# Last down products in column halves, and attention's small loads on the weights' queue

## The chip, the cores and the metric

One core of a Trainium2 chip runs the whole program. The metric is the device time of one execution in microseconds (us); three runs of the kernel before took 1378.57, 1380.28 and 1381.85, the median being 1380.28. The engines are TensorE (PE; PEld is its weight load), VectorE (DVE), ScalarE (ACT), GpSimd (POOL) and SyncE (SP), which here issues transfers. Each engine works through its own stream of instructions in order, and they meet at semaphores.

## The reference

Two pre-norm residual layers on x of 256 tokens by 1024 columns, with adaLN: for each layer, six vectors of 1024 (two shifts, two scales, two gates) come from `silu(c) @ ada_w + ada_b`.

```python
h = rmsnorm(x, norm_mix_w[layer]) * (1.0 + sc1) + sh1
y = hybrid_mixer(h, ...) if layer % 2 == 0 else diff_attention(h, ...)
x = x + g1 * y
h = rmsnorm(x, norm_ffn_w[layer]) * (1.0 + sc2) + sh2
f = swiglu(h, ...) if layer % 2 == 0 else moe_swiglu(h, ...)   # 8 experts, top 2
x = x + g2 * f
```

Layer 0 has the mixer (gated DeltaNet and S5) and a dense SwiGLU with D_FF = 2816; layer 1 has differential attention and the experts. Attention uses a few small parameters: weights of 64 for the norms of q and k (q also takes 1/8), a weight of 128 for the norm of the output times 1 - lambda_init, and

```python
lam = exp(sum(lq1 * lk1)) - exp(sum(lq2 * lk2)) + lambda_init   # four vectors of 64
p = softmax(s1) - lam * softmax(s2)                              # per head, chunk-causal mask
```

## The kernel before

The program is one long list of instructions, written stage by stage; a planner then orders each engine's stream by its own estimate of when operands are ready and by priorities. `behind(ins)` adds an edge for the planner alone: what is written inside comes after `ins` on the engine of `ins`. `modnorm` and `residual` are written with a high priority.

*Weights.* `raw` (L105) issues a load of 1 MB on SP into one of nine buffers, and the load waits until that buffer is free. `split` (L118) makes a high part (whi, ScalarE, L131) and a low part (wlo, VectorE, L132) of 1024 columns; each product of float32 is done as three products of such parts (L398 to L400 for the projections with weights stationary, L406 to L408 for those with tokens stationary).

*Dense feed-forward* (`dense_ffn`). The 22 blocks of 128 hidden columns (f) run in order: two projections of 24 products each, silu and the product of both, the split of the result (hfT, L1162 and L1163), and, one block later, the down products into four accumulators `acc[tt][n]` (two blocks of 128 tokens by two halves of 512 columns; 12 products for each f). Blocks 20 and 21 are left for one last call of `down`, whose 24 products are written token block by token block. Beside this, VectorE sums chunks of the adaLN weights (`ada_sums`, L280 and L282), which TensorE folds in small products (L301). Then `residual_` is called for eight pieces of 256 columns, token block by token block: VectorE multiplies the accumulator by the gate (L733) and adds to x (L734), and ScalarE takes the squares with their sum (L318).

*Norm* (`modnorm_`). VectorE reduces the sums of squares (sst, L332), GpSimd takes the power (L157, L158), x is scaled into xn (L370, L371), TensorE transposes it (tr, L150), ScalarE applies scale and shift (hf, L385), and VectorE splits this into hT (L387, L388), two of the eight steps of 128 at a time. `self.later` holds the last instruction of ScalarE and of VectorE in this.

*Attention* (`diff_attention`). Ahead of its norm it loads small parameters on ScalarE's queue: four rows into rowsC, then subln, four vectors into lt, and the mask, ten transfers in all; the sums on them follow each load at once (a transpose of rowsC and two copies to wcol, L1190 and L1191; subln times a constant, L1194; four instructions for lambda on VectorE, L1199 to L1205, with an Exp on ScalarE, L1202). The tiles are in the pool that takes the place of the feed-forward's. Then come the norm, the projections of q, k and v, adaLN chunks (one on TensorE, L272; its bias rows adab on SP, L295), the heads and the output projection, woven together by due times. The expert stage follows, with most of the weights.

Of the kernel before, what the change touches and what calls it, by code (L numbers as in the profile page):

```python
# [17 lines left out]
P = 128  # L18
T = 256
NT = 2  # L20
# [54 lines left out]
class Trunk:  # L75
# [326 lines left out]
    def tok3(self, out, hT, k, tt, wh, wl, first, last):  # L402
# [5 lines left out]
        nc.tensor.matmul(out, hT[:, k, 0, s], wl, start=False, stop=last)  # L408
# [718 lines left out]
    def dense_ffn(self):  # L1127
# [8 lines left out]
        def down(steps):  # L1136
            self.mark("ffn_down")
            parts = [self.split(w, D) for f, hf, w in steps]
            for tt in range(NT):
# [32 lines left out]
        down(wait)  # L1172
        for tt in range(NT):
            for n in range(4):
                self.residual(acc[tt][n // 2][:, (n % 2) * 256:(n % 2) * 256 + 256], self.gates[(0, 1)], tt,
                              slice(256 * n, 256 * n + 256))


    def diff_attention(self):
# [4 lines left out]
        for r, n in enumerate(("odd_q_norm_w", "odd_k_norm_w")):  # L1184
            for i in range(2):
                S.dma_start(rC[r:r + 1, i, :], a[n])
        pt = self.ps("ms")
        self.transpose(pt[:, :2], rC.rearrange("r i d -> r (i d)"))
        wcol = ap.tile([P, 2], F32, name="wcol")
        V.tensor_scalar(wcol[:, 0:1], pt[:, 0:1], 0.125, None, op0=ALU.mult)  # L1190
        V.tensor_copy(wcol[:, 1:2], pt[:, 1:2])  # L1191
        sub = ap.tile([P, P], F32, name="subln")
        S.dma_start(sub, a["odd_subln_w"].to_broadcast([P, P]))
        V.tensor_scalar(sub, sub, 1.0 - LAMBDA_INIT, None, op0=ALU.mult)  # L1194
        lt = ap.tile([P, 4, 64], F32, tag="ex", name="lt", bufs=2)
        for i, n in enumerate(("odd_lambda_q1", "odd_lambda_k1", "odd_lambda_q2", "odd_lambda_k2")):
            S.dma_start(lt[:, i, :], a[n].to_broadcast([P, 64]))
        lp = ap.tile([P, 2, 64], F32, tag="ex", name="lp", bufs=2)
        V.tensor_tensor(lp, lt[:, 0::2, :], lt[:, 1::2, :], op=ALU.mult)  # L1199
        ls = ap.tile([P, 2], F32, name="lsum")  # L1200
        V.tensor_reduce(ls, lp, axis=AX.X, op=ALU.add)
        S.activation(ls, ls, AF.Exp)  # L1202
        nlam = ap.tile([P, 1], F32, name="nlam")
        V.tensor_tensor(nlam, ls[:, 1:2], ls[:, 0:1], op=ALU.subtract)
        V.tensor_scalar(nlam, nlam, -LAMBDA_INIT, None, op0=ALU.add)  # L1205
        msk = ap.tile([P, T], F32, name="amask")
        S.dma_start(msk, a["amask"])
        hT, _, _ = self.modnorm(1, 0, ap, ("oT",))
        yT = ap.tile([P, KD, 2, T], F32R, name="oT", tag="oT")
# [627 lines left out]
```

## Time and profile before

| | before |
|---|---|
| time of the profiled execution | 1378.09 us |
| its span, first to last instruction | 1376.3 us |
| median of the timed runs | 1380.28 us |
| mean granted TensorE clock | 0.978 |
| TensorE, VectorE, ScalarE busy | 1281.9, 826.4, 577.1 us |
| read from HBM | 398.11 MB |

The busy time of an engine is the time in which at least one of its instructions ran. The granted clock is the share of TensorE's full speed that the throttle let through. DMA is the mean busy share of 16 DMA engines. The words after an arrow in a row name what ended the idle time ahead of that instruction.

### The profile page before, as it was taken

To read this page: it belongs to the slowest core of one execution; us is meant where nothing else is said; L and a number is where in the kernel's file an instruction comes from. 1 tells how busy PE (TensorE), PEld (TensorE's weight loads), DVE (VectorE), ACT (ScalarE), POOL (GpSimd) and SP (SyncE) were. 2 spreads that over 40 slices of the span, in tenths; PEclk is the share of its full clock that TensorE was granted. 3 is DMA by queue.
4 is the path that set the end of the run, shared out by engine and by line. 5 is a ranking of instruction groups with operands and counts; after the bars stand their busy time and mean duration, and the time that the engine had idled before them with its cause. 6 is when DMAs were issued, how large, how long until landed. Compare 5 with 4: busy or idle time off the path is not lost.

```text
span 1376.3 us, 26749 instructions
## 1 busy us (share of the span) xinstructions
PE 1281.9 (93%) x10928; PEld 941.8 (68%) x10928; DVE 826.4 (60%) x1516; ACT 577.1 (42%) x990; POOL 123.6 (9%) x118
## 2 busy tenths in 40 slices
PE   3999999989999978999999999999998899999975
PEld 2777666779999978998788435786352468835334
DVE  6688767567878878965798413986020089820202
ACT  3553322455444444664778213775010168711000
POOL 3132322000000003341100000000000000000000
PEclk9799999999999999999999999999999999999998
DMA  9834334159788967821899899999999999999995
GB/s 262 268 114 132 111 106 154 62 177 325 247 270 287 293 211 252 271 96 63 334 305 399 305 380 409 405 409 356 391 409 405 408 409 406 409 397 408 408 396 208
DMA packets 196164, 400.98 MB, mean 291 GB/s; under 512 B 14797, under 2 KB 115650, under 8 KB 196034
## 3 DMA queue, kind: packets, MB, share of 16 engines
q1 hardware_dynamic: 189610, 398.00, 78.7%
q10 hardware_dynamic: 6424, 1.19, 0.5%
q8 instruction: 88, 1.44, 0.4%
q14 instruction: 42, 0.34, 0.1%
HBM read 398.11 MB, written 1.05 MB: 290 GB/s over the span
## 4 chain that ended last, share of the span: by engine, by line
PE 46%; DMA 10%; DVE 4%; issue 1%; ACT 1%; SPq 1%; POOL 0%; ACTq 0%; DVEq 0%
PE pab L1731 9%; DMA raw<-in_odd_expert_w 9%; PE py L1782 5%; PE pab L1675 4%; PE pab L1674 4%; PE pab L1676 4%; PE py L1708 2%; PE py L1709 2%; PE py L1707 2%; PE px L1625 2%; DVE wlo L132 1%; PE pqk L398 1%; PE pqk L399 1%; PE pqk L400 1%; PE pth L150 1%
## 5 line engine op out<-in xcount | busy, mean ns | idle before, releaser
L131 ACT ACTIVATE whi<-raw 128x1024 fp32r<-128x1024 f32 (+2 forms) x352 | 347.1, 1001 | 279.8 <-PE pab L399 52.3
L132 DVE TENSOR_TENSOR wlo<-raw,whi 128x1024 fp32r<-128x1024 f32 (+2 forms) x352 | 402.9, 1168 | 72.6 <-ACT whi L131 70.6
L1731 PE MATMUL pab<-raw,xg 128*32 128x512 f32 (+1 forms) x1920 | 194.2, 524 | 10.5 <-DMA raw<-in_odd_expert_w 10.5
L1731 PEld LDWEIGHTS pab<-raw,xg 128*32 128x32 f32 x1920 | 58.2, 109 | 118.8 <-issue 77.5
L1751 DVE TENSOR_TENSOR hb<-hb,pab 128x256 f32<-128x256 f32 (+1 forms) x35 | 12.4, 364 | 171.0 <-ACT hb L1750 170.5
L1675 PE MATMUL pab<-wlo,xg 128*128 128x512 f32 (+1 forms) x288 | 110.3, 383 | 3.6 <-DVE wlo L132 3.4
L1676 PE MATMUL pab<-whi,xg 128*128 128x512 f32 (+1 forms) x288 | 106.4, 377 | 0.0
L398 PE MATMUL pab<-hT,whi 128*128 128x256 f32 x352 | 101.9, 290 | 0.0
L399 PE MATMUL pab<-hT,whi 128*128 128x256 f32 x352 | 100.3, 285 | 0.1
L400 PE MATMUL pab<-hT,wlo 128*128 128x256 f32 x352 | 99.9, 284 | 0.0
L1782 PE MATMUL py<-raw,hTe 128*32 128x256 f32 (+1 forms) x1760 | 83.7, 343 | 10.7 <-DMA raw<-in_odd_expert_w 8.6
L282 DVE SCALAR_TENSOR_TENSOR adas<-raw,condr,adas 128x256 f32<-128x256 f32 x175 | 86.4, 499 | 3.1
L1674 PE MATMUL pab<-whi,xg 128*128 128x512 f32 (+1 forms) x288 | 84.4, 379 | 3.6 <-DVE xg L1632 1.9
L1782 PEld LDWEIGHTS py<-raw,hTe 128*32 128x32 f32 x1760 | 53.4, 112 | 38.0 <-DMA raw<-in_odd_expert_w 12.8
L1802 DVE TENSOR_TENSOR yf<-py,gate 32x256 f32<-32x256 f32 (+1 forms) x48 | 18.0, 374 | 102.3 <-PE py L1782 101.3
L1750 ACT ACTIVATE hb<-pab 128x256 f32<-128x256 f32 (+1 forms) x35 | 11.5, 338 | 155.8 <-PE pab L1731 155.1
L399 PEld LDWEIGHTS pab<-hT,whi 128*128 128x128 f32 x352 | 68.0, 193 | 0.8 <-DVE hT L388 0.5
L398 PEld LDWEIGHTS pab<-hT,whi 128*128 128x128 f32 x352 | 68.1, 193 | 0.3
L400 PEld LDWEIGHTS pab<-hT,wlo 128*128 128x128 f32 x352 | 67.9, 193 | 0.1
L1675 PEld LDWEIGHTS pab<-wlo,xg 128*128 128x128 f32 x288 | 54.3, 189 | 19.4 <-DVE wlo L132 6.3
L1676 PEld LDWEIGHTS pab<-whi,xg 128*128 128x128 f32 x288 | 54.4, 189 | 10.0
L1674 PEld LDWEIGHTS pab<-whi,xg 128*128 128x128 f32 x288 | 51.0, 189 | 13.7 <-ACT whi L131 2.2
(465 smaller groups left out, 2504.4 us busy)
## 6 DMA issues: line engine op xcount, KB each, us to landing
raw<-in_odd_expert_w SPq DMA_DIRECT2D x215, 1024.0 KB
raw<-in_ada_w SPq DMA_DIRECT2D x48, 1024.0 KB
raw<-in_odd_expert_w SPq DMA_DIRECT2D x64, 768.0 KB
raw<-in_even_ffn_w SPq DMA_DIRECT2D x33, 1024.0 KB
raw<-in_odd_w_qkv SPq DMA_DIRECT2D x12, 1024.0 KB
raw<-in_even_w_in SPq DMA_DIRECT2D x10, 1024.0 KB
raw<-in_even_w_out SPq DMA_DIRECT2D x4, 1024.0 KB
raw<-in_odd_w_out SPq DMA_DIRECT2D x4, 1024.0 KB
```

The costliest lines, as they stand in the source:

```text
L131: act = nc.scalar.activation(hs, src, AF.Copy)
L132: dve = nc.vector.tensor_tensor(l, src, hs, op=ALU.subtract)
L282: nc.vector.scalar_tensor_tensor(s, w[:, k, :], self.condr[:, k, 0:1], s, op0=ALU.mult, op1=ALU.add)
L398: nc.tensor.matmul(out, wh[:, o:o + P], hT[:, k, 0, :], start=(k == 0), stop=False)
L399: nc.tensor.matmul(out, wh[:, o:o + P], hT[:, k, 1, :], start=False, stop=False)
L400: nc.tensor.matmul(out, wl[:, o:o + P], hT[:, k, 0, :], start=False, stop=(k == kd - 1))
L1625: PE.matmul(px[:, kk * n:kk * n + n], self.xn[:, tt, k * P:(k + 1) * P], Pt[:, tt, :n], start=(tt == 0), stop=(tt == 1))
L1674: PE.matmul(p[:, :m], xg[:, k, 0, :], wh[:, s], start=(k == 0), stop=False)
L1675: PE.matmul(p[:, :m], xg[:, k, 0, :], wl[:, s], start=False, stop=False)
L1676: PE.matmul(p[:, :m], xg[:, k, 1, :], wh[:, s], start=False, stop=(k == KD - 1))
L1731: PE.matmul(pu[t][32 * g:32 * g + 32], xg[:, k, 32 * t:32 * t + 32], v[:, :, g * n:(g + 1) * n], start=(k == 0 and (t == 0 or n > P)), sto ...
L1782: PE.matmul(py[32 * g:32 * g + 32, t], hs[f][t], v[:, i, g * n:(g + 1) * n], start=(f == 0 and t == 0), stop=(f == NF - 1 and t == 1))
```

## The change

In `dense_ffn`, the last call of `down` is made with `halves`: the products of columns 0 to 511 of blocks 20 and 21, for both token blocks, and then those of columns 512 to 1023, the second half written behind the last product of the first. The eight pieces of the residual follow in the same order: the four of the first half, then the four of the second. In `diff_attention` the ten small transfers are issued on SP's queue, and all the sums on them are gathered in `small()`, which is called after the norm and behind `self.later`, so that its ScalarE and VectorE instructions come after the norm's last ones on these engines. `wcol` and `nlam` become tiles made after the norm. `tok3` returns its last product.

```diff
-        nc.tensor.matmul(out, hT[:, k, 0, s], wl, start=False, stop=last)
+        return nc.tensor.matmul(out, hT[:, k, 0, s], wl, start=False, stop=last)
...
-        def down(steps):
+        def down(steps, halves=False):
             self.mark("ffn_down")
             parts = [self.split(w, D) for f, hf, w in steps]
+            if halves:
+                mm = None
+                for n in range(2):
+                    cs = slice(512 * n, 512 * n + 512)
+                    with self.behind([mm.ins] if mm else ()):
+                        for (f, hf, w), (wh, wl) in zip(steps, parts):
+                            for tt in range(NT):
+                                mm = self.tok3(acc[tt][n], hf, 0, tt, wh[:, cs], wl[:, cs], f == 0, f == NF - 1)
+                return
...
-        down(wait)
-        for tt in range(NT):
-            for n in range(4):
-                self.residual(acc[tt][n // 2][:, (n % 2) * 256:(n % 2) * 256 + 256], self.gates[(0, 1)], tt,
-                              slice(256 * n, 256 * n + 256))
+        down(wait, True)
+        for h in range(2):
+            for tt in range(NT):
+                for n in (2 * h, 2 * h + 1):
+                    self.residual(acc[tt][h][:, (n % 2) * 256:(n % 2) * 256 + 256], self.gates[(0, 1)], tt,
+                                  slice(256 * n, 256 * n + 256))
...
-                S.dma_start(rC[r:r + 1, i, :], a[n])
+                nc.sync.dma_start(rC[r:r + 1, i, :], a[n])
...
-        S.dma_start(sub, a["odd_subln_w"].to_broadcast([P, P]))
-        V.tensor_scalar(sub, sub, 1.0 - LAMBDA_INIT, None, op0=ALU.mult)
+        nc.sync.dma_start(sub, a["odd_subln_w"].to_broadcast([P, P]))
...
-            S.dma_start(lt[:, i, :], a[n].to_broadcast([P, 64]))
+            nc.sync.dma_start(lt[:, i, :], a[n].to_broadcast([P, 64]))
...
-        S.dma_start(msk, a["amask"])
+        nc.sync.dma_start(msk, a["amask"])
         hT, _, _ = self.modnorm(1, 0, ap, ("oT",))
+        wcol, nlam = ap.tile([P, 2], F32, name="wcol"), ap.tile([P, 1], F32, name="nlam")
+
+        def small():
+            pt = self.ps("ms")
+            self.transpose(pt[:, :2], rC.rearrange("r i d -> r (i d)"))
+            V.tensor_scalar(wcol[:, 0:1], pt[:, 0:1], 0.125, None, op0=ALU.mult)
+            V.tensor_copy(wcol[:, 1:2], pt[:, 1:2])
+            V.tensor_scalar(sub, sub, 1.0 - LAMBDA_INIT, None, op0=ALU.mult)
+            lp = ap.tile([P, 2, 64], F32, tag="ex", name="lp", bufs=2)
+            V.tensor_tensor(lp, lt[:, 0::2, :], lt[:, 1::2, :], op=ALU.mult)
+            ls = ap.tile([P, 2], F32, name="lsum")
+            V.tensor_reduce(ls, lp, axis=AX.X, op=ALU.add)
+            S.activation(ls, ls, AF.Exp)
+            V.tensor_tensor(nlam, ls[:, 1:2], ls[:, 0:1], op=ALU.subtract)
+            V.tensor_scalar(nlam, nlam, -LAMBDA_INIT, None, op0=ALU.add)
+
+        with self.behind(self.later):
+            small()
```

## Rows read from the trace of the kernel before

**Rows 1.** The page: busy time of each engine with its share of the span and its instructions, and the chain of work that ended last by engine.

```profile
PE 1281.9 (93%) x10928; PEld 941.8 (68%) x10928; DVE 826.4 (60%) x1516; ACT 577.1 (42%) x990; POOL 123.6 (9%) x118
...
PE 46%; DMA 10%; DVE 4%; issue 1%; ACT 1%; SPq 1%; POOL 0%; ACTq 0%; DVEq 0%
```

**Rows 2.** The table by stretches of time: the stretch in us, its length, then busy us and instructions of PE, PEld, DVE, ACT and POOL, the granted clock, the DMA share and GB/s.

```profile
503.00:509.70 6.70, 0.00 (x0) 0.00 (x0) 4.77 (x15) 5.32 (x19) 0.89 (x2) 0.74 0.01 4
517.40:521.10 3.70, 0.00 (x0) 0.00 (x0) 0.65 (x3) 3.68 (x4) 0.00 (x0) 0.84 0.79 264
521.10:526.60 5.50, 5.25 (x23) 4.96 (x24) 5.50 (x13) 1.92 (x4) 0.00 (x0) 0.50 0.23 67
526.60:550.00 23.40, 22.98 (x194) 22.16 (x194) 21.37 (x39) 8.86 (x14) 10.54 (x8) 1.00 0.95 309
550.00:585.00 35.00, 34.29 (x281) 31.88 (x281) 31.96 (x91) 21.26 (x57) 12.47 (x15) 1.00 0.83 268
526.60:668.00 141.40, 138.02 (x1131) 127.51 (x1130) 101.98 (x284) 79.61 (x203) 43.61 (x48) 0.99 0.55 179
760.00:1376.00 616.00, 571.61 (x5618) 337.58 (x5617) 251.83 (x329) 204.09 (x292) 0.00 (x0) 0.99 0.99 385
```

**Rows 3.** TensorE's instructions in order of time at the feed-forward's last products: start, duration, line, operands. The first row is the first of the last 24, the second the twelfth, the third the small adaLN products between the blocks, the last row the last of the 24.

```profile
496.65 0.48 PE L406 MATMUL facc<-whi,hfT 128*128 128x512 f32 x1
...
499.27 0.39 PE L408 MATMUL facc<-wlo,hfT 128*128 128x512 f32 x1
499.50 0.50 PE L301 MATMUL gvb<-ones,adas 128*128 128x1 f32 x4
...
502.50 0.39 PE L408 MATMUL facc<-wlo,hfT 128*128 128x512 f32 x1
```

**Rows 4.** VectorE in order of time, same place: the low part of the last hfT, the first two and the last two instructions of the residual.

```profile
497.87 0.43 DVE L1163 TENSOR_TENSOR hfT<-h,hfT 128x256 fp32r<-128x256 f32 x1 [0.41 <-ACT hfT L1162]
...
501.55 0.76 DVE L733 TENSOR_TENSOR res<-facc,gate 128x256 f32<-128x256 f32 x2 [1.15 <-PE facc L408]
...
506.21 0.76 DVE L734 TENSOR_TENSOR x<-x,res 128x256 f32<-128x256 f32 x2
```

**Rows 5.** VectorE in order of time at attention's norm: the reduction, the first cast, the sums on subln, wcol and lt with their waits in brackets, the last instruction of hT, and the low part of the second column's weights.

```profile
507.81 0.16 DVE L332 TENSOR_REDUCE sst<-ss 128x2 f32<-128x8 f32 x1 [0.84 <-ACT sqj L318]
...
512.36 0.43 DVE L387 CAST hT<-hf 128x512 fp32r<-128x512 f32 x1 [1.28 <-ACT hf L385]
514.21 0.23 DVE L1194 TENSOR_SCALAR subln<-subln 128x128 f32<-128x128 f32 x1 [1.42 <-DMA subln<-in_odd_subln_w]
...
515.28 0.15 DVE L1190 TENSOR_SCALAR wcol<-ps 128x1 f32<-128x1 f32 x1
...
520.45 0.29 DVE L1199 TENSOR_TENSOR lp<-lt 128x128 f32<-128x128 f32 x1 [4.35 <-DMA lt<-in_odd_lambda_k]
...
522.31 0.69 DVE L388 TENSOR_TENSOR hT<-hf,hT 128x512 fp32r<-128x512 f32 x1
...
523.45 1.22 DVE L132 TENSOR_TENSOR wlo<-raw,whi 128x1024 fp32r<-128x1024 f32 x1
```

**Rows 6.** The same norm at the head of the feed-forward stage, in order of time: the reduction and the last instruction of hT on VectorE, the transposes on TensorE, the first four hf on ScalarE.

```profile
300.54 0.16 DVE L332 TENSOR_REDUCE sst<-ss 128x2 f32<-128x8 f32 x1 [0.84 <-ACT sqj L318]
...
308.99 0.69 DVE L388 TENSOR_TENSOR hT<-hf,hT 128x512 fp32r<-128x512 f32 x1
...
302.54 3.65 PE L150 MATMUL tr<-cst,xn 128*128 128x128 f32 x16 [4.68 <-ACT xn L371]
...
304.09 1.93 ACT L385 ACTIVATE hf<-tr,modc,modc 128x256 f32<-128x256 f32 x4 [0.96 <-PE tr L150]
```

**Rows 7.** The table by stretches for the products of L398 alone, one of the three in each step of a projection: length, busy us and number on PE and PEld, clock, DMA share, GB/s. The first stretch is the start of the feed-forward, the second that of attention.

```profile
305.00:312.00 7.00, 4.12 (x13) 3.05 (x13) 0.76 1.07 367
514.00:526.60 12.60, 4.31 (x12) 3.25 (x12) 0.73 0.36 114
```

**Rows 8.** TensorE in order of time: the adaLN chunk at the start of attention.

```profile
513.40 1.07 PE L272 MATMUL gv<-raw,condr 128*32 128x256 f32 x16
```

**Rows 9.** SP in order of time: when it issued its transfers (where a row holds several, from the first's start to the last's end).

```profile
469.04 10.75 SPq L110 DMA_DIRECT2D raw<-in_odd_w_qkv  x3
...
486.94 6.15 SPq L110 DMA_DIRECT2D raw<-in_ada_w  x3
496.06 0.37 SPq L110 DMA_DIRECT2D raw<-in_odd_w_qkv  x1
507.85 0.25 SPq L295 DMA_DIRECT2D adab<-in_ada_b  x1
514.53 0.38 SPq L110 DMA_DIRECT2D raw<-in_ada_w  x1
...
545.12 4.48 SPq L110 DMA_DIRECT2D raw<-in_odd_w_qkv  x2
```

**Rows 10.** ScalarE in order of time at attention's norm: the issues of subln and of the last of lt (ACTq) and, between them, the third and fourth hf.

```profile
511.32 0.35 ACTq L1193 DMA_DIRECT2D subln<-in_odd_subln_w  x1
...
512.22 1.02 ACT L385 ACTIVATE hf<-tr,modc,modc 128x256 f32<-128x256 f32 x2
...
513.16 0.44 ACTq L1197 DMA_DIRECT2D lt<-in_odd_lambda_k  x1
```

More of the change, by code (lines that the diff above doesn't have):

```diff
@@ L1185, in diff_attention @@
             for i in range(2):
-                S.dma_start(rC[r:r + 1, i, :], a[n])
[L1187 to L1191, printed above, removed]
+                nc.sync.dma_start(rC[r:r + 1, i, :], a[n])
         sub = ap.tile([P, P], F32, name="subln")
-        S.dma_start(sub, a["odd_subln_w"].to_broadcast([P, P]))
@@ L1194, in diff_attention @@
-        V.tensor_scalar(sub, sub, 1.0 - LAMBDA_INIT, None, op0=ALU.mult)
+        nc.sync.dma_start(sub, a["odd_subln_w"].to_broadcast([P, P]))
         lt = ap.tile([P, 4, 64], F32, tag="ex", name="lt", bufs=2)
         for i, n in enumerate(("odd_lambda_q1", "odd_lambda_k1", "odd_lambda_q2", "odd_lambda_k2")):
-            S.dma_start(lt[:, i, :], a[n].to_broadcast([P, 64]))
-        lp = ap.tile([P, 2, 64], F32, tag="ex", name="lp", bufs=2)
-        V.tensor_tensor(lp, lt[:, 0::2, :], lt[:, 1::2, :], op=ALU.mult)
@@ L1200, in diff_attention @@
[L1200 to L1205, printed above, removed]
+            nc.sync.dma_start(lt[:, i, :], a[n].to_broadcast([P, 64]))
         msk = ap.tile([P, T], F32, name="amask")
-        S.dma_start(msk, a["amask"])
+        nc.sync.dma_start(msk, a["amask"])
```

## The prediction

> **What bounds the kernel now.** I began with the page [rows 1]: TensorE is busy for 93% of the span, and the chain that ended last goes 46% over TensorE and 10% over DMA. Since such shares mix stages, I next read a table by stage [rows 2]: from 760 us on DMA is at 0.99, so the expert stage ends when its weights have come, and from 526.6 to 668 TensorE works for 138.0 of 141.4 us. Between the dense feed-forward and attention there is a hole: TensorE does nothing in 503.0 to 509.7 and in 517.4 to 521.1, and behind the second of these idle times, in 521.1 to 526.6, its granted clock is 0.50 (1.2 of 2.4 GHz). The change lies in that hole. Third I read the instructions there in order of time, and the reader is to see three things: the residual on VectorE, eight pieces from 501.55 to 506.97, begins when the last products are nearly done [rows 3, 4]; VectorE then stands still twice, 1.42 us for subln and 4.35 us for lt, in the middle of the casts to hT [rows 5]; and the same norm at the head of the feed-forward stage, with nothing small in it, takes far less [rows 6].
>
> The profiled execution took 1378.09 us, 1.8 us more than its span; the median of the three timed runs, 1380.28, is 2.19 above it. I sum against the first and add the 2.19.
>
> **Residuals by halves.** The last 24 products run as f=20 over four accumulators and then f=21 over four, so all four close late, the last at 502.89 [rows 3]. In the new order the 12 products of columns 0 to 511 come first; the first 12 of now end at 499.66 [rows 3], and so would these. The low part of hfT, which f=21 needs, is there at 498.30 [rows 4]; the six products of f=20 last until about 498.0, and high products stand ready for the rest, so the order costs TensorE nothing that I can see. VectorE is idle then and does the first four pieces at 0.67 us each (eight in 501.55 to 506.97 [rows 4]), until 502.2. Half 1 still ends on TensorE at 502.89, its first token block three products (0.7 us) earlier. From 502.2 the other four pieces take 2.8 us: the last x stands at 505.0 in place of 506.97. **Gain 2.0 us**; the reduction of the squares moves from 507.81 to 505.8. Bounds: if both blocks of half 1 close only at 502.89, 1.3; if the small products at 499.50, 0.36 us to the start of the next product at 499.86, move behind half 1, 2.4. The ordering edge lies within TensorE's own stream and makes nothing else wait.
>
> **The norm without the sums.** Before, attention needs 526.6 - 507.81 = 18.8 us from the reduction to the end of the slow stretch, by which TensorE has done 12 steps of three products [rows 5, 7]. The feed-forward norm has 13 steps by 312.0, so 12 by about 311.6, 11.1 us after its reduction at 300.54 [rows 6, 7]. It too starts from an idle TensorE (4.68 us [rows 6]), with a mean clock of 0.76 over these steps, so the price of the clock is in its time. Attention has TensorE work that the other has not: 16 products of an adaLN chunk, 1.07 us [rows 8], four small ones, 0.36, and a transpose, together 1.5 us. Charged in full: 18.8 - 11.1 - 1.5 = **6.2 us gained**; if they fit between products that wait for hT, 7.7. Check from the other side: hT is whole at 523.0, 15.2 us from the reduction, the feed-forward's at 309.68, 9.14 us; the 6.05 between are the two waits, 5.77, and sums done among the casts [rows 5, 6].
>
> What hides the loads: SP can issue them when the last square has freed the feed-forward's tiles, as its adab load did at 507.85 [rows 9], so now near 505.9. Ten issues of 0.25 to 0.44 us and the gaps between them make 3.6 us, until 509.5; adab is pushed back by as much, and the weight load behind it waits for a buffer anyway (it went out at 514.53 [rows 9]). The transpose of the norm weights needs the first four, asked for 4 us before its turn. A small load was usable 2.5 us after its issue had ended (subln, 511.67 to 514.21 [rows 5, 10]).
>
> The seven sums on VectorE, 1.4 us by their own durations (0.15 to 0.29 [rows 5]), now stand behind hT, and the low part of the second column's weights (at 523.45 [rows 5]) behind them. That column is due when TensorE has done the first and the 1.5 us already charged, so they are hidden; uncovered they cost 1.4. lt was usable 6.8 us after its last issue had ended (513.60 to 520.4 [rows 5, 10]); by that it comes at 516.3, while hT is whole at 505.8 + 9.14 = 514.95: a wait of 0 to 1.3. I take 0.3, since 3.7 us of the old landing lay beside a weight load (DMA 0.79 [rows 2]) that now comes later. ScalarE's Exp with its table load stays, behind the last hf.
>
> A page speaks against half of this. On ScalarE the issues cost nothing: two hf took 1.02 us among them, four took 1.93 in the feed-forward without any [rows 6, 10]. The Trainium skill (DMA: Bandwidth & Descriptors, "Issuing engines are not separate DMA queues") says that starting transfers from other engines saves only the sequencer's time to start them; the trace agrees, and by that rule alone the change of queue would be worth 0 in place of the 6.2, which rest on the earlier issue and on where the sums stand. The same page ("Queues, rings and completion order") has each DMA engine take a ring's descriptors in order, so that a small load on the weights' queue begins behind weights already there; in 503.0 to 509.7 DMA stands at 0.01 and 4 GB/s [rows 2], so there should be none.
>
> **Does it carry to the end?** From 526.6 to 668 TensorE is idle for 3.4 us only [rows 2], so attention is a fixed amount of work after its start; VectorE has 91% of 550 to 585 and moves along, since its waits stood ahead of that. The expert stage begins behind attention's last products, and its stream of weights, which bounds the rest, with it. Sum: 2.0 + 6.2 - 0.3 = 7.9; 1378.09 - 7.9 + 2.19 = **1372.4**.
>
> **The rivals.**
> (a) *lt late again.* If the sums are put directly behind hT and the loads lie behind others on SP, VectorE waits behind the norm instead of in it. For: the old run shows 4.35 us of just this wait. Against: the issue comes 4 us earlier against hT. Price: 4.35 in place of 0.3, a gain of 3.85: 1376.4.
> (b) *The shift is swallowed later.* For: DMA has 0.95 of 526.6 to 550 [rows 2], and a planner orders anew all that follows. Against: these loads start on buffers that compute frees. Price: all of it, 1379 to 1381.
> (c) *Slower: head of the line on SP.* The ten are traced ahead of attention's weights. If the planner puts them in front of the loads that went out from 469.04 to 496.06 (five of w_qkv, three of ada_w, the last three from 486.94 on), these wait for the feed-forward's tiles, until 509.5. Then 17 loads that were all issued by 549.6 [rows 9] must come after it, at 2.72 us each (1 MB at the 385 GB/s of [rows 2]) 46.3 us, with 2.5 until the first is usable 558.3, against 552.1 before: 6.2 us later. It decides from about the sixth load held back: five cost 13.6 us, which DMA's idle time after 509 takes up. Against: adab waits for the same tiles and was put behind all eight. Half of the worst, 1383.4, stands for it.
> That the halves come out undone, a gain of 5.9, stays inside the forecast.
>
> **How the numbers follow.** Forecast 0.62, (a) 0.16, (b) 0.13, (c) 0.09. The forecast's own range: gains from 2.4 + 7.7 = 10.1 to 1.3 + 6.2 - 1.3 - 1.4 = 4.8 give 1370.2 to 1375.5, and with the timed runs' spread of 1.6 either way 1368.6 to 1377.1. The range of 8 in 10 takes in (a) and the near part of (b): 1368.6 to 1379.5. What a measurement can tell from no change is 0.2%, 2.8 us, so below 1377.5 is faster: the forecast and most of (a), 0.76; same 0.15, from (b) and the rest of (a); slower 0.09.
>
> **What would show it.** In the new trace: the products of half 0 all before those of half 1, the first residual near 499.3 and the reduction near 505.8; the ten loads on SP from 505.9; no wait of VectorE for a load between the first cast to hT and the last, which ends 9.1 us after the reduction; the twelfth step of the first projection 12.6 us after it. I would be wrong if SP's w_qkv loads go out later than before, if VectorE waits for lt longer than 1.3 us, or if the first expert products come 8 us earlier and the end does not.

## The result and the profile after

The changed kernel takes **1371.89 us** (median of four runs, 1369.30 to 1372.85), the kernel before 1381.07 beside it: a ratio of 0.9927, 95% interval 0.9905 to 0.9950. Ten more runs, beside others of the kernel before, gave 1374.22 against 1381.29, 0.9946 [0.9927, 0.9965]. The profiled execution took 1371.06 us with a span of 1369.3 and a mean granted clock of 0.979 (before: 1378.09, 1376.3, 0.978).

The page of the kernel after: busy time of each engine, and the chain that ended last by engine.

```profile
PE 1280.6 (94%) x10928; PEld 940.7 (69%) x10928; DVE 828.6 (61%) x1516; ACT 578.3 (42%) x990; POOL 121.9 (9%) x118
...
PE 48%; DMA 8%; DVE 2%; ACT 1%; issue 1%; POOL 0%; ACTq 0%; DVEq 0%
```

Against [rows 1] the busy times stay within 2.2 us of what they were and the span is 7.0 us shorter: most of what went is idle time. In the kernel before the chain begins at 507.78, behind the residual, and holds the load of lt for 7.10 us (513.16 to 520.26); in the kernel after it has no piece before 535. The fall of VectorE's share from 4% to 2% is no sign of the change: up to 535 VectorE has 1.4 us of the chain before, but 13.9 us in 850 to 900, in the expert stage, where it has none in the chain after.

TensorE of the kernel after, in order of time (start, duration, line, operands): the first of the last 24 products, the small adaLN products, the last of the 24, the transposes of attention's norm with the idle time ahead of them, and the adaLN chunk.

```profile
496.90 0.47 PE L406 MATMUL facc<-whi,hfT 128*128 128x512 f32 x1
...
498.37 0.50 PE L301 MATMUL gvb<-ones,adas 128*128 128x1 f32 x4
...
502.68 0.39 PE L408 MATMUL facc<-wlo,hfT 128*128 128x512 f32 x1
508.18 3.65 PE L150 MATMUL tr<-cst,xn 128*128 128x128 f32 x16 [5.11 <-ACT xn L371]
...
511.95 1.87 PE L272 MATMUL gv<-raw,condr 128*32 128x256 f32 x16
```

VectorE of the kernel after, same stretch: the first two and the last two instructions of the residual, the reduction, the first cast to hT, the last instruction of hT, the sums on wcol, subln and lt, and the low part of the next weights.

```profile
499.93 0.76 DVE L733 TENSOR_TENSOR res<-facc,gate 128x256 f32<-128x256 f32 x2 [0.67 <-PE facc L408]
...
504.60 0.75 DVE L734 TENSOR_TENSOR x<-x,res 128x256 f32<-128x256 f32 x2
506.19 0.16 DVE L332 TENSOR_REDUCE sst<-ss 128x2 f32<-128x8 f32 x1 [0.84 <-ACT sqj L318]
...
510.78 0.43 DVE L387 CAST hT<-hf 128x512 fp32r<-128x512 f32 x1 [1.31 <-ACT hf L385]
...
514.63 0.69 DVE L388 TENSOR_TENSOR hT<-hf,hT 128x512 fp32r<-128x512 f32 x1
515.24 0.15 DVE L1210 TENSOR_SCALAR wcol<-ps 128x1 f32<-128x1 f32 x1
...
515.38 0.22 DVE L1212 TENSOR_SCALAR subln<-subln 128x128 f32<-128x128 f32 x1
515.51 0.28 DVE L1214 TENSOR_TENSOR lp<-lt 128x128 f32<-128x128 f32 x1
...
515.97 1.22 DVE L132 TENSOR_TENSOR wlo<-raw,whi 128x1024 fp32r<-128x1024 f32 x1
```

SP of the kernel after, its issues in order of time: the last load of w_qkv ahead of the norm, the first of the small ones, the last of lt, the mask, the adaLN bias and the next weights.

```profile
496.31 0.37 SPq L110 DMA_DIRECT2D raw<-in_odd_w_qkv  x1
506.24 0.55 SPq L1196 DMA_DIRECT2D rowsC<-in_odd_q_norm_w  x2
...
509.24 0.43 SPq L1201 DMA_DIRECT2D lt<-in_odd_lambda_k  x1
509.71 0.43 SPq L1203 DMA_DIRECT2D amask<-in_amask  x1
510.19 0.29 SPq L295 DMA_DIRECT2D adab<-in_ada_b  x1
513.88 0.38 SPq L110 DMA_DIRECT2D raw<-in_ada_w  x1
```

The reader is to see three things against [rows 3 to 5]. The residual starts at 499.93, while half of the last products are still to run, and its eight pieces follow each other without a gap. From the first cast to the last instruction of hT no row of VectorE carries a wait in brackets, where it waited 1.42 and 4.35 us before. And lp, the first sum on lt, carries no wait in brackets: lt is there when its turn comes. SP's weight loads keep their places [rows 9]; the small ones took the place in which only adab stood.

To place gains and losses I cut each profile at the same five instructions: the start of ScalarE's last silu of the feed-forward (496.55 before, 496.80 after), the reduction of the squares, ScalarE's first copy into kT (the second column of the projection), the last product of the router's logits (the end of attention's TensorE work), and the last store. The numbers are differences of those starts in us. The stretch before the silu is left out, because the change doesn't touch it: from the reduction at the head of the feed-forward to that silu every profile of this document takes 196.0 us, except one that is named below.

| profile | silu to reduction | reduction to kT | kT to logits | logits to store | silu to kT | silu to logits | silu to store |
|---|---|---|---|---|---|---|---|
| before | 11.26 | 24.46 | 130.6 | 707.9 | 35.7 | 166.3 | 874.2 |
| before, again | 11.26 | 24.53 | 130.6 | 708.3 | 35.8 | 166.4 | 874.7 |
| after | 9.40 | 18.21 | 131.9 | 708.0 | 27.6 | 159.5 | 867.4 |
| after, again | 9.39 | 18.17 | 131.9 | 709.2 | 27.6 | 159.4 | 868.6 |

Between silu and kT these two programs repeat themselves within 0.1 us. That isn't so for every kernel: two profiles of the halves alone, below, differ by 1.1 there, in how long VectorE waits for lt. Behind kT differences of one to three are met between profiles of one program.

### The profile page after: what moved, and what is told of

Same layout as the page of the kernel before. It is cut to its first block, busy times and chain, and to the rows that moved or that the text cites. A ratio compares the mean times of both kernels' runs of the same rounds, so it can differ in the third digit from the quotient of the medians.

```text
span 1369.3 us, 26750 instructions
## 1 busy us (share of the span) xinstructions
PE 1280.6 (94%) x10928; PEld 940.7 (69%) x10928; DVE 828.6 (61%) x1516; ACT 578.3 (42%) x990; POOL 121.9 (9%) x118
## 4 chain that ended last, share of the span: by engine, by line
PE 48%; DMA 8%; DVE 2%; ACT 1%; issue 1%; POOL 0%; ACTq 0%; DVEq 0%
PE pab L1745 9%; DMA raw<-in_odd_expert_w 8%; PE py L1796 6%; PE pab L1689 5%; PE pab L1688 5%; PE pab L1690 5%; PE py L1722 2%; PE py L1723 2%; PE py L1721 2%; PE px L1639 2%; PE pth L150 1%; DVE yf L1816 1%; DVE wlo L132 1%; PE psc L1823 1%; PE psc L1310 1%; PE psc L1824 1%
## 5 line engine op out<-in xcount | busy, mean ns | idle before, releaser
L398 PE MATMUL pab<-hT,whi 128*128 128x256 f32 x352 | 101.9, 290 | 0.0
L398 PEld LDWEIGHTS pab<-hT,whi 128*128 128x128 f32 x352 | 68.0, 193 | 0.3
```

Of the source, the lines that this page charges most:

```text
L398: nc.tensor.matmul(out, wh[:, o:o + P], hT[:, k, 0, :], start=(k == 0), stop=False)
```

## The experiments

My theory: the gain has two independent parts ahead of kT (residual 2.0, norm 6.2), the second of which comes from SP's earlier issue and from the sums' place behind the norm together, and all of it is carried to the end. The rivals: the queue alone does it or does nothing; lt is late again; the shift is swallowed behind kT; loads held back on SP cost more than all that. All times are beside runs of the kernel before on the same chip:

| kernel | median us | before | ratio [95%] |
|---|---|---|---|
| after, again | 1374.22 | 1381.29 | 0.9946 [0.9927, 0.9965] |
| halves alone | 1381.76 | 1379.85 | 1.0013 [0.9991, 1.0034] |
| halves alone, again | 1380.13 | 1379.53 | 1.0013 [0.9992, 1.0034] |
| attention's part alone | 1375.72 | 1379.85 | 0.9969 [0.9949, 0.9988] |
| loads on ScalarE's queue, sums behind the norm | 1377.25 | 1379.85 | 0.9979 [0.9962, 0.9997] |
| loads on SP, sums ahead of the norm | 1378.96 | 1379.85 | 0.9990 [0.9970, 1.0009] |
| loads on ScalarE's queue, sums further back | 1374.70 | 1379.53 | 0.9972 [0.9947, 0.9997] |
| w_qkv held behind the small loads | 1388.92 | 1381.29 | 1.0053 [1.0026, 1.0080] |
| adaLN chunk behind the first column | 1375.68 | 1381.29 | 0.9968 [0.9945, 0.9990] |
| loads and sums in the feed-forward | 1382.90 | 1381.29 | 1.0011 [0.9983, 1.0040] |
| products in TensorE's hole | 1374.07 | 1379.53 | 0.9958 [0.9939, 0.9977] |

And the same cuts in their profiles:

| profile | silu to reduction | reduction to kT | kT to logits | silu to kT | silu to logits | silu to store |
|---|---|---|---|---|---|---|
| halves alone | 9.39 | 24.50 | 135.2 | 33.9 | 169.0 | 878.8 |
| halves alone, again | 9.39 | 23.41 | 132.2 | 32.8 | 165.0 | 874.5 |
| attention's part alone | 11.26 | 17.94 | 132.9 | 29.2 | 162.1 | 870.9 |
| ScalarE's queue, behind the norm | 9.39 | 22.77 | 130.9 | 32.2 | 163.1 | 871.0 |
| SP, sums ahead | 9.39 | 20.18 | 132.2 | 29.6 | 161.8 | 875.5 |
| ScalarE's queue, further back | 10.49 | 17.76 | 131.4 | 28.2 | 159.6 | 875.6 |
| w_qkv held | 9.39 | 27.33 | 140.7 | 36.7 | 177.4 | 885.6 |
| chunk behind first column | 9.39 | 17.82 | 134.9 | 27.2 | 162.1 | 871.1 |
| loads and sums early | 10.50 | 17.79 | 133.1 | 28.3 | 161.4 | 870.3 |
| products in the hole | 9.39 | 18.15 | 134.3 | 27.5 | 161.8 | 870.6 |

### Each part alone

The feed-forward's part alone is the kernel before with

```diff
-        down(wait)
-        for tt in range(NT):
-            for n in range(4):
+        down(wait, True)
+        for h in range(2):
+            for tt in range(NT):
+                for n in (2 * h, 2 * h + 1):
```

> The feed-forward part alone (products and residuals by halves), attention's head as before. Theory of the prediction (two separate gains that add): the reduction of the squares comes 1.6 to 2.0 us earlier (near 506.1), the two waits of VectorE for subln and lt stay (1.4 and 4.4 us, within 1), hT is whole 15 us after the reduction, the first qT at 524.2 against 525.9, and the span is 1.5 to 2 us shorter, 1374.3 to 1374.8. Rival (the gain is the planner's new order of what follows, not the hole): the span moves by something that the first qT does not show.

and, later, once more, with a second profile of the kernel before beside it:

> The feed-forward part alone, once more. In its first profile the 1.9 us gained at the first kT were gone again at the logits (135.2 us from kT to the logits against 130.5 before), with three drops of the granted clock between. Theory A (the drops belong to the execution, not to the order of instructions): this profile has them elsewhere or not at all, and kT to the logits takes 130.5 to 132. Theory B (the new order of attention costs it): again 134 to 136, at a full clock too.

> The kernel before, profiled once more. Theory A (drops of the clock belong to the execution): the segments before the change and behind it move by some us with the clock, while from the last silu to the first kT it is 35.8 us again, within 0.5. Theory B: every segment repeats within 0.3 us.

Attention's part alone is the kernel after with these lines as they were before.

> Attention's part alone (loads on SP, sums behind the norm), the feed-forward's end as before. Theory of the prediction: the reduction stays at 507.8, no wait of VectorE between the first and the last cast, hT whole 9.1 us after the reduction (516.9), the first qT near 519.8, 6.1 us earlier than before, and the span 5.3 to 6 us shorter, 1370.3 to 1371.0. Rival as in the run of halves alone: first qT and span don't go together.

The halves bring the reduction 1.9 us forward (11.26 to 9.39, twice), attention's part leaves it (11.26) and brings kT forward by 6.5 us in all. At kT the parts give 1.8 (2.9 in the second profile) and 6.5; 1.8 and 6.5 make 8.3, 2.9 and 6.5 make 9.4, and the change has 8.1. So they add up there as far as single profiles can tell. The waits remain where attention is as before. VectorE of the halves alone, again, in order of time (the wait for lt was 4.13 in the first profile, as forecast, and here 2.82):

```profile
512.88 0.23 DVE L1204 TENSOR_SCALAR subln<-subln 128x128 f32<-128x128 f32 x1 [1.67 <-DMA subln<-in_odd_subln_w]
...
517.60 0.29 DVE L1209 TENSOR_TENSOR lp<-lt 128x128 f32<-128x128 f32 x1 [2.82 <-DMA lt<-in_odd_lambda_k]
```

In the time of the whole program the halves alone can't be seen, twice (1.0013). Both profiles lose their gain behind kT: kT to logits is 4.6 us longer than before in the first and 1.6 in the second. The first has a granted clock of 0.97 over that stretch, the second 1.00 as before, so the clock can account for the excess of the first and not for the 1.6 of the second. Attention's part alone keeps 4.1 of its 6.5 to the logits, and its time says 0.9969. At the end of the program the parts are therefore not shown to add: the intervals of attention's part alone and of the whole change overlap, and no run shows that the halves shorten the whole time.

### Queue and place of the sums

The queue alone is undone by

```diff
-                nc.sync.dma_start(rC[r:r + 1, i, :], a[n])
+                S.dma_start(rC[r:r + 1, i, :], a[n])
...
-            nc.sync.dma_start(lt[:, i, :], a[n].to_broadcast([P, 64]))
+            S.dma_start(lt[:, i, :], a[n].to_broadcast([P, 64]))
```

and likewise for subln and the mask; the sums stay behind the norm.

> The changed kernel with its ten loads back on ScalarE's queue, the sums still behind the norm. Theory A (the place of the sums is what counts, the queue is worth nothing): hf at the same distances (about 0.46 us), hT whole 9.1 us after the reduction, span within 1 us of the changed kernel's 1369.3. Theory B (late landing, the first rival): in ScalarE's stream the loads stand between xn and hf, so the last of lt is issued near 511.7 in place of 509.7, lands 6.8 us later, near 518.4, and VectorE waits for it behind the norm, 2 to 3 us before the low part of the second column; the first qT 2 us later, span near 1371.5. Theory C (the issues on ScalarE hold up hf): hT whole 11 to 12 us after the reduction.

ScalarE's issues and VectorE's instructions of this kernel, in order of time: the last issue of lt; then the last of hT, the sum on subln, the first on lt.

```profile
509.98 0.44 ACTq L1201 DMA_DIRECT2D lt<-in_odd_lambda_k  x1
...
513.13 0.69 DVE L388 TENSOR_TENSOR hT<-hf,hT 128x512 fp32r<-128x512 f32 x1
...
513.87 0.22 DVE L1212 TENSOR_SCALAR subln<-subln 128x128 f32<-128x128 f32 x1
516.99 0.29 DVE L1214 TENSOR_TENSOR lp<-lt 128x128 f32<-128x128 f32 x1 [2.90 <-DMA lt<-in_odd_lambda_k]
```

hT is whole nearly as early as in the kernel after (9.46 us behind the reduction, there 9.13), so the issues between ScalarE's hf cost 0.3 us at most. But ScalarE gets to the issues of lt only behind its part of xn and among the hf: the last ends at 510.42, 2.7 us before the last hT starts; in the kernel after it ends at 509.67, 5.0 before. VectorE then waits 2.90 us for lt, with the low part of the second column's weights queued behind it. TensorE waits 3.2 us for that low part, its granted clock is 0.75 in 516.4 to 521.0 against 1.00 in the 4.4 us ahead, and kT comes 4.6 us later (32.2 against 27.6). This is my rival (a), made real.

The other half is undone by calling `small()` ahead of the norm, with the loads on SP:

```diff
-        hT, _, _ = self.modnorm(1, 0, ap, ("oT",))
...
-        with self.behind(self.later):
-            small()
+        small()
+        hT, _, _ = self.modnorm(1, 0, ap, ("oT",))
```

> The changed kernel with the sums written ahead of the norm again, the loads still on SP. Theory A (place of the sums): VectorE meets lp among the casts near 513 while lt has not landed (issue ends 509.7; by 6.8 us it lands at 516.5), waits up to 3 us there, hT whole 12 us after the reduction, the first qT 2 to 3 us later, span 1371.5 to 1372.5. Theory D (the earlier issue is what counts, by itself): lt lands before 513, no wait above 0.5 us, hT whole 10 us after the reduction, span within 1 us of 1369.3.

SP's last issue of lt in this kernel, and VectorE: the sums on subln and lt and the last of hT.

```profile
510.49 0.43 SPq L1201 DMA_DIRECT2D lt<-in_odd_lambda_k  x1
...
511.56 0.23 DVE L1211 TENSOR_SCALAR subln<-subln 128x128 f32<-128x128 f32 x1 [0.84 <-DMA subln<-in_odd_subln_w]
...
515.67 0.29 DVE L1213 TENSOR_TENSOR lp<-lt 128x128 f32<-128x128 f32 x1 [2.02 <-DMA lt<-in_odd_lambda_k]
...
518.20 0.69 DVE L388 TENSOR_TENSOR hT<-hf,hT 128x512 fp32r<-128x512 f32 x1
```

The waits are back among the casts, 0.84 and 2.02 in place of 1.42 and 4.35, and hT is whole 11.44 us behind the reduction. Reduction to kT: 24.46 before, 20.18 with SP alone, 22.77 with the sums' place alone, 18.21 with both. Of the 6.25 us the earlier issue alone brings 4.3, the later use alone 1.7, from one profile each.

Is it then the queue, or the time between issue and use? The last kernel of this group leaves the loads on ScalarE's queue and puts the sums behind the low part of the second column's weights:

```diff
-        with self.behind(self.later):
-            small()
...
+                        if (hp, kind) == (0, 0):
+                            with self.behind(self.lastsplit):
+                                small()
```

> The ten loads on ScalarE's queue as in the run with the loads back there, but the sums on them placed further on, behind the low part of the second column's weights. It tells why ScalarE's queue cost 3.6 us there. Theory A (only because VectorE waited 2.90 us for lt in front of the second column's low part): the issues are as late as there (last of lt 21 us after the last silu of the feed-forward), VectorE's wait for lt is under 1 us, the first kT is back to 27.6 to 28.2 us after that silu (32.1 there) and the logits near 159.5 to 160. Theory B (the issues themselves, between xn and hf, cost ScalarE): first kT stays above 31.

ScalarE's last issue of lt, and VectorE's last of hT and first sum on lt:

```profile
508.38 0.44 ACTq L1201 DMA_DIRECT2D lt<-in_odd_lambda_k  x1
...
511.65 0.69 DVE L388 TENSOR_TENSOR hT<-hf,hT 128x512 fp32r<-128x512 f32 x1
...
514.19 0.29 DVE L1214 TENSOR_TENSOR lp<-lt 128x128 f32<-128x128 f32 x1
```

The wait is gone with the old queue. kT stands at 28.2, and the logits at 159.6 against the kernel after's 159.5. The 0.6 at kT has a reason apart from the queue: the planner moved the adaLN chunk (1.07 us on TensorE) between the last products, so that the reduction comes 1.1 later (10.49 against 9.40). Since the order differs in this, the price of the queue by itself isn't isolated to better than some tenths. It costs nothing that these profiles can show; what costs is a sum that meets a load still in flight. (Behind the logits this profile loses 8.0 us more, at a granted clock of 0.98 against 0.99 in the second half of the expert stage; the medians say 0.9972.)

### Loads held back on SP

Rival (c) was made real by writing every load of w_qkv behind the last small one:

```diff
-        nc.sync.dma_start(msk, a["amask"])
+        lastsmall = [nc.sync.dma_start(msk, a["amask"]).ins]
...
+                with self.behind(lastsmall):
+                    raws = {kind: self.raw(wq[:, D * kind + 256 * hp:D * kind + 256 * hp + 256].rearrange("(k p) n -> p k n", p=P),
+                                           (KD, 256)) for kind in kinds}
```

> The changed kernel with all loads of w_qkv set behind the ten small loads on SP; by SP's order the adaLN loads between them are held back too, nine loads of 1 MB in all. It makes the slower rival (c) real and tests its price. By (c): none of the nine before 510, then 2.7 us each; the first product of the projection near 517 in place of 513.7; the stage loses against the changed kernel what the backlog of loads is late, 12 to 14 us by the logits, so 5 to 7 us slower than before (span near 1382). Other theory (DMA's idle time takes up the backlog): only the start, 3 to 4 us, is lost, span near 1373.

SP of this kernel in order of time: the last weight loads ahead, the mask, and the first of w_qkv. A second fence has TensorE's first product of the projection, a third the table by stretches (columns as in [rows 2]) up to that product and just behind it.

```profile
468.08 3.27 SPq L110 DMA_DIRECT2D raw<-in_ada_w  x2
...
514.57 0.42 SPq L1203 DMA_DIRECT2D amask<-in_amask  x1
515.04 1.06 SPq L110 DMA_DIRECT2D raw<-in_odd_w_qkv  x2
```

```profile
525.62 0.58 PE L398 MATMUL pqk<-hT,whi 128*128 128x256 f32 x1 [8.77 <-ACT whi L131]
```

```profile
516.90:525.60 8.70, 0.00 (x0) 0.00 (x0) 3.89 (x12) 3.11 (x6) 0.00 (x0) 0.50 0.83 275
525.60:529.10 3.50, 3.33 (x14) 3.04 (x15) 2.76 (x5) 3.47 (x5) 0.00 (x0) 0.50 1.10 349
```

SP issued nothing in 471.4 to 511.1, and TensorE then stood 8.77 us for weights. Against the kernel after, kT comes 9.1 us later and the logits 18.0, where 12 to 14 were expected; against the kernel before 11.1 at the logits, and 7.6 in the medians (interval 3.6 to 11.0; the prediction had 6.2). So the danger was real and its sign right. The price was too small at the logits; in the whole time 6.2 lies within the interval. I had priced the end of a queue of loads, but the first product already paid, and at the lower granted clock of 0.50 behind the long idle time. The count was off as well: a load of ada_w at 480.87 was left out, so from 469.04 to 496.06 nine loads went out, not eight, and 18 until 549.6, not 17. By the prediction's own working that makes 8.9 us in place of 6.2.

### Three that could have beaten it

*The adaLN chunk behind the first column.* The prediction charged 1.5 us for work that attention's start has and the feed-forward's has not. Putting the chunk (1.87 us in the kernel after, at the lower clock) behind the first column tests that:

```diff
+            with self.behind(self.firstcol or ()):
...
+                            mm = self.proj_T(pp[:, :T], hT, wh, wl, 0, P)
+                            if self.firstcol is None:
+                                self.firstcol = [mm.ins]
```

> The changed kernel with attention's one adaLN chunk on TensorE (16 products) set behind the first column of the projection. It tests the 1.5 us that the prediction charged in full. Theory A (charged rightly, TensorE has no free time while hT comes): the first kT as in the changed kernel, 18.2 us after the reduction, within 0.3. Theory B (the products fit into TensorE's waits for hT, the upper bound of 7.7 in place of 6.2): the first product of the projection 11.95 to 12.2 instead of 13.74 (6 us after the reduction instead of 7.5) and the first kT 1 to 1.5 us earlier, 16.7 to 17.2 us after the reduction.

TensorE of this kernel, in order of time: the transpose of the norm weights and, at once, the first product.

```profile
509.98 0.26 PE L150 MATMUL ps<-cst,rowsC 2*128 2x2 f32 x1
510.17 0.58 PE L399 MATMUL pqk<-hT,whi 128*128 128x256 f32 x1
```

The first product stands 5.72 us behind the reduction against 7.55, but kT gains only 0.4 (27.2 against 27.6): just past the 0.3 of theory A and far from the 1 to 1.5 of theory B. The first products now run at the lower clock in the chunk's place (0.41 us each for some, 0.28 later), and the chunk, 1.07 us, stands between the two columns, still ahead of kT. Behind the transposes TensorE waits for nothing but 0.2 us for a low part, so its work is what sets kT. The time, 0.9968, is not below the kernel after's.

*Loads and sums in the feed-forward.* The small tiles get a pool of their own, loads and sums stand behind block 6 of the feed-forward, and only the Exp and the last two instructions on nlam stay behind the norm:

```diff
+            self.attsm = asm.enter_context(tc.tile_pool(name="attsm", bufs=1))
...
+                if f == 6:
+                    self.small_loads()
```

> The changed kernel with the ten loads and all sums but the last Exp and lambda's two steps moved into the feed-forward stage, in a small pool of their own (block 6). It tests whether loads and sums still cost anything behind the norm. Theory A (they are hidden, as the prediction took it, at 0.3): first kT 18 us after the reduction, nothing gained beyond 0.3 us. Theory B (the 1.4 us of sums or a rest of a wait for lt stand on the path): the low part of the second column 0.7 us or more earlier against hT, the first kT 0.7 to 1.7 us earlier, 16.5 to 17.5 us after the reduction.

A miss: nothing of attention's norm waits for a small load any more, and yet kT comes 0.7 us later than in the kernel after. As with the sums further back, the adaLN chunk lies between the last products and delays the reduction by 1.1 (10.50 against 9.40). Then ScalarE, in order of time, puts the Exp's table load ahead of weights for which TensorE waits 1.4 us:

```profile
518.03 1.28 ACT L1227 ACT_TABLE_LOAD   x1
519.32 0.20 ACT L1227 ACTIVATE lsum<-lsum 128x2 f32<-128x2 f32 x1
519.43 3.89 ACT L131 ACTIVATE whi<-raw 128x1024 fp32r<-128x1024 f32 x4
```

The time is that of the kernel before (1.0011), 8.7 us above the kernel after's in the medians. From silu to store the profile is 1.7 to 2.9 us longer. More lies ahead of the silu, where the table doesn't look: the planner put the loads and the sums at the start of the feed-forward's blocks, and VectorE waits for lt there:

```profile
324.55 0.29 DVE L1216 TENSOR_TENSOR lp<-lt 128x128 f32<-128x128 f32 x1 [3.26 <-DMA lt<-in_odd_lambda_k]
```

From the feed-forward's own reduction to its last silu this profile takes 199.6 us, where the thirteen others take 196.0. So the wait was moved rather than hidden, into a stage where TensorE has nothing to spare (busy for 190.9 us of 305 to 496 before). These parts make 5.3 to 6.5 of the 8.7; the rest stays open.

*Products in the hole.* TensorE still stands idle for 5.1 us ahead of the transposes. Here 20 products of 128x512 from weights already in place, into a tile that nothing reads, are put there, and the transposes behind them, which adds work and changes no output:

```diff
+                with self.behind([mm.ins]):
+                    for i in range(self.NWARM):
+                        mm = nc.tensor.matmul(pw, wh[:, :P], wh[:, 512:1024], start=True, stop=True)
```

> The changed kernel with 20 products of 128x512 added behind the last down product, into a PSUM tile that nobody reads: 4.6 us of work in TensorE's 5.1 us of idle time. It tests what the granted clock costs in the hole. Theory A (the transposes and the adaLN chunk run at 1.2 GHz because TensorE was idle before them): the clock stays at 1.0 through the norm, the 16 transposes take 2 us or less in place of 3.65, the first hf 0.5 to 0.8 us earlier, hT whole 8.3 to 8.6 us after the reduction in place of 9.1, the first kT 0.7 to 1.2 us earlier (26.4 to 26.9 after the silu). Theory B (the clock there costs nothing since ScalarE and VectorE set the pace): kT unchanged within 0.3.

The table by stretches: the kernel after ahead of the transposes and during them,

```profile
503.10:508.20 5.10, 0.03 (x1) 0.06 (x1) 3.16 (x10) 4.13 (x13) 0.89 (x2) 0.86 0.01 4
508.20:512.00 3.80, 3.80 (x21) 3.45 (x25) 2.45 (x5) 2.52 (x5) 0.00 (x0) 0.50 0.16 40
```

the kernel with the added products from the last silu to kT,

```profile
495.80:523.40 27.60, 24.78 (x169) 21.50 (x169) 21.82 (x53) 19.16 (x41) 0.89 (x2) 1.00 0.59 188
```

and its VectorE at the first sum on lt:

```profile
515.24 0.29 DVE L1223 TENSOR_TENSOR lp<-lt 128x128 f32<-128x128 f32 x1 [1.10 <-issue]
```

In the kernel after the transposes run at a granted clock of 0.50 (1.2 of 2.4 GHz) behind the idle time; with the added products it is 1.00 throughout, the first product comes 2.6 us earlier behind the reduction (4.97 against 7.55) and hT is whole 0.5 earlier (8.65). kT doesn't move: VectorE stands still for 1.10 ahead of the first sum on lt, and TensorE waits 1.9 us for the low part that follows it. The row names no releaser; that it is lt, 6.54 us after its last issue, is likely by the other kernels, but not shown. The time, 0.9958, has an interval that covers the 0.9946 of the kernel after. No version tried here is clearly faster than the kernel after.

And the kernel after once more, for its spread:

> The changed kernel once more, beside the next three on the same chip. All theories: the reduction 9.4 us after the last silu of the feed-forward, hT whole 9.1 us after it, the first kT 27.6 us after that silu (35.8 before), the logits 131 to 132 us after the first kT. If the spread of the timed runs comes from the granted clock, the runs with the lower mean clock are the longer ones, about 0.9 us for each 0.001; if it comes from the order of instructions, it does not follow the clock.

## Why the prediction was right

*The residual by halves: 2.0 forecast, 1.87 measured* (11.26 to 9.40 and 9.39). The first residual came at 499.93, later than the 499.3 named: 0.25 is the later start of the whole stretch, and the small adaLN products, 0.36 us, stood in the midst of half 0, where I had left them between the halves. The eight pieces follow without a gap and take 5.4 us, so the first one sets the reduction: 506.19 in place of 505.8, of which 0.25 is the later start and the rest the shortfall.

*The norm without the sums: 6.2 forecast, 6.25 measured* (24.46 to 18.21). hT is whole 9.13 us behind the reduction, against the 9.14 that I took from the feed-forward's norm [rows 6]. Carrying over the same norm from another stage was the best single step. Charging the 1.5 us of attention's extra TensorE work in full was nearly right: no product waits for hT any more, and moving the chunk gave back 0.4. The twelve steps, by the products of L398 (length, busy us and number on PE and PEld, clock, DMA share, GB/s), last until 12.5 us behind the reduction, 12.6 forecast:

```profile
512.50:518.70 6.20, 3.07 (x12) 2.17 (x12) 0.91 0.67 206
```

*lt: a wait of 0.3 forecast, none seen.* From the end of its last issue lt took at most 5.8 us (509.67 to 515.51). Where a wait shows when it could be used, that was 4.75 us after it (sums ahead, 510.92 to 515.67), 6.57 (ScalarE's queue), 6.85 before, and 6.62 and 4.48 in the two profiles of the halves alone, one unchanged program. So the kernel after, which uses lt 5.8 us after the issue in both its profiles, has no sure margin: with the same loads on SP, VectorE waits 0.32 for lt in the kernel with the chunk behind the first column and 0.68 in the one with w_qkv held. That no wait at all came is in part luck; the bounds of 0 to 1.3 were fair. Rival (a) is what happens with 2.3 us less between issue and use (2.7 against 5.0).

*The queue as such.* The Trainium skill (DMA: Bandwidth & Descriptors, "Issuing engines are not separate DMA queues") says that starting transfers from several engines saves only the sequencer's time to start them. The runs agree as far as the issues' own cost goes: with the sums far enough back, the old queue stands at 159.6 us at the logits against 159.5. But the engine also decides when the issue comes, and with the sums directly behind the norm that was worth 4.6 us at kT.

*Does it carry? This is the step that was mis-sized.* I let the whole 7.9 go to the end. At kT there are 8.1; at the logits 6.8; in the spans 7.0. The missing 1.3 lies between kT and logits: 130.6 in both profiles before, 131.9 in both after. The table by stretches of the kernel before, and then of the kernel after:

```profile
532.30:662.80 130.50, 127.98 (x1048) 119.52 (x1046) 93.24 (x254) 72.09 (x195) 43.61 (x48) 1.00 0.52 170
```

```profile
524.40:656.30 131.90, 128.71 (x1049) 120.35 (x1047) 94.25 (x257) 72.64 (x196) 42.05 (x48) 1.00 0.51 169
```

TensorE is idle for 3.2 us in place of 2.5 and busy for 0.7 longer with the same work. The waits of TensorE in that stretch of the kernel after (total us, times, longest) have two that before has not, 0.3 for kT and this one:

```profile
PE gvb L297 <- POOL adas L296: 0.7, 1, 0.7
```

That names the idle half: TensorE reaches an adaLN chunk ahead of GpSimd's addition to it. Both profiles of the halves alone have that wait too (0.6), and the kernel with the old queue has not and takes 130.9. The other 0.7 is spread over a thousand products, less than 1 ns each on average, and its cause stays open. So rival (b) was true for a sixth of the gain, through the planner's new order rather than through DMA.

*The expert stage* moved along as forecast: logits to store is 707.9 and 708.3 us before, 708.0 and 709.2 after.

*The sum.* 7.9 us forecast, 7.0 in the profiles, 9.2 and 7.1 in two pairs of medians; 1372.4 against 1371.89 and 1374.22. The nearness of the first is partly luck: the profiled execution gained 0.9 less than forecast (7.0 against 7.9), and the median of the four runs lies 0.8 above it, where the prediction had added 2.19. The two errors, of 0.9 and 1.4, have opposite signs. Those four runs had a mean granted clock of 0.980, the ten 0.979.

What stays open: why the halves alone, worth 1.9 us at the reduction in every kernel whose last products hold no adaLN chunk, give nothing at the end of theirs. They lose it behind kT, where the planner's order differs; no run here isolates which difference it is.

## What to carry to other kernels

A small parameter costs by the distance between its issue and its first use, and by what is queued behind the instruction that uses it: put the use behind the stretch that everything waits for, and ask which instruction of which engine's stream lets the issue go. A load moved to an earlier stage brings its wait along, if its use is moved too and follows it closely. The price of a stretch cleared of such waits can be read from a like stretch elsewhere in the same trace, here to a tenth of a microsecond. Where a planner orders what follows, count on a gain of a few microseconds changing by one or two behind the place where it was made, and read it at several fixed instructions, not at the end alone.

## What the runs showed of the hardware

The kernels before and after repeat themselves from silu to kT within 0.1 us, and the feed-forward from its reduction to its last silu takes 196.0 us in thirteen profiles, and yet whole times differ by much more than the change is worth: the kernel before took 1373.47 to 1391.13 us in the comparisons, at mean granted clocks of 0.981 and 0.969. A line through all timed runs, with a level of its own for each kernel, falls by 0.93 us for each 0.001 of mean clock. The place where the clock falls changes from run to run with unchanged code. The table by stretches for 167 to 190 us, first of one profile of the kernel after and then of the other:

```profile
167.00:190.00 23.00, 23.00 (x158) 14.93 (x158) 15.68 (x32) 3.78 (x13) 3.47 (x2) 0.93 0.28 92
```

```profile
167.00:190.00 23.00, 23.00 (x148) 14.39 (x146) 13.53 (x26) 3.19 (x8) 2.92 (x3) 0.78 0.28 93
```

TensorE is busy throughout in both, the clock is 0.93 in one and 0.78 in the other; the last silu comes at 496.8 and 501.2. A change of some 2 us, such as the halves alone, is therefore read from fixed places within the profile rather than from the time.

A small load doesn't repeat itself as well: in two profiles of one program lt could be used 6.62 and 4.48 us after its last issue had ended, and kT moved by 1.1 us with it.
